# Ending a hand-made section ahead of the last store, with a second engine waiting for the earlier stores

## The chip, the cores and the metric

The kernel runs on one core of one Trainium2 chip. The metric is the device time in microseconds (us) of one execution. Every kernel here was executed several times, and its median is quoted. The record marks all executions quoted as fast: none lies over 1.5% above the fastest of its kernel. The profile of a kernel is that of one execution; its "span" runs from the first to the last instruction and is about 2 us shorter than the measured time.

## The reference

Sixteen independent products of a transposed 512 x 512 matrix with another, in float32:

```python
def setup_inputs():
    batch, m, k, n = 16, 512, 512, 512
    return {"a": randn(batch, k, m), "b": randn(batch, k, n)}       # float32

def reference(a, b):
    return np.matmul(a.transpose(0, 2, 1), b).astype(np.float32)
```

Inputs and outputs together are 50.33 MB: 33.55 MB are read and 16.78 MB written.

## The kernel before

The kernel takes two of the sixteen products at a time ("pairs", eight of them). SyncE issues all the DMAs, on one queue: sixteen loads of 2 MB, then eight stores of 2 MB. VectorE casts to bf16, TensorE multiplies, ScalarE copies the results from PSUM to the output tiles. The fifth engine, GpSimd, has no part in the products. All of this stands in one hand-made section (`tile_critical`), in which the author places every semaphore (a counter that one engine or DMA raises and another waits for); outside such a section the framework places them. The parts that matter here:

```python
    NX = 4                       # load buffers
    NO = pairs - 1               # 7 output tiles for 8 pairs
    ...
    with tc.tile_critical(no_gpsimd_drain=True):
        for n in range(2 * pairs):
            if n >= NX:
                nc.sync.wait_ge(s_in, n - NX + 1)
            nc.sync.dma_start(x_ts[n % NX][:], in_v[n % 2][n // 2]).then_inc(s_x[n % NX], 16)
        for i in range(pairs):
            nc.sync.wait_ge(s_out, i + 1)
            nc.sync.dma_start(out_v[i], o_ts[i % NO][:]).then_inc(s_o if i else s_o0, 16)
        nc.sync.wait_ge(s_o0, 16)                  # the waits at the section's end
        nc.sync.wait_ge(s_o, 16 * (pairs - 1))
        ...                                        # VectorE: casts; TensorE: matmuls
        for i in range(pairs):
            if i == NO:
                nc.scalar.wait_ge(s_o0, 16)        # store 0 has left its tile
            ...                                    # ScalarE: copies of PSUM to o_ts[i % NO]
            nc.scalar.memzero(act_done[:, i:i + 1]).then_inc(s_out, 1)
```

When a section ends, the framework adds an exit. In the compiled program of this kernel, SyncE announces that it has left; TensorE, VectorE, ScalarE and SyncE each drain (wait until their own earlier work is done) when they see this, and answer; SyncE collects the four answers. Then come the program's last instructions: a drain on SyncE that waits for what is still outstanding, and two rounds of a barrier of all engines with the clearing of the semaphores between them.

## Time and profile before

| | before |
|---|---|
| time, median of 3 runs | 124.58 us (124.52 to 124.60) |
| span of the profiled run | 122.5 us |
| bytes moved, mean rate over the span | 50.33 MB, 411 GB/s |
| share of the span in which the DMA engines are busy | 97.3% |
| last compute instruction ends | 94.5 us |
| last store complete ("last landing") | 121.11 us |
| from there to the end of the span ("tail") | 1.40 us |

A DMA here runs on sixteen DMA engines, and each of them adds one to the DMA's semaphore when its share is done. "Landing" below is always the moment of the sixteenth. The prediction shows the lines of this profile that carry the argument, with how to read them. In rows such as `L71 SPq EVENT_SEMAPHORE  x1: 17/17/17, 121.1 to 121.1` the three numbers are the shortest, median and longest duration in nanoseconds, and the last two the start of the first and the last of the group in microseconds; a q after the engine's name marks its sequencer. These views round to 0.1 us. Where I give more digits, they are start times and completion times of the same trace, which holds nanoseconds.

### The profile page before, as it was taken

The numbers are of one execution on the slowest core, as the hardware profiler recorded it, in microseconds if no ns is written. First come the engines' busy times: TensorE is split into PE (matmuls) and PEld (weight loads), VectorE is DVE, ScalarE is ACT, GpSimd is POOL, SyncE is SP. The second block draws the span as 40 slices with busy tenths as digits, with TensorE's granted clock in tenths as the row PEclk, the third lists the DMA queues.
The fourth block names the chain that finished last, engine by engine and source line by source line (L and its number), as shares of the span: only waits on it lengthen the run. The fifth ranks groups of instructions, "written<-read, shape, count | busy, mean of one in ns | idle before, by whom it ended". The sixth has DMA issues, their size and how long they took to land. (4 is left out here: it accounts for less than half of the span.)

```text
span 122.5 us, 1252 instructions
## 1 busy us (share of the span) xinstructions
PE 62.0 (51%) x512; PEld 35.8 (29%) x512; DVE 37.9 (31%) x48; ACT 31.8 (26%) x41; POOL 0.2 (0%) x4
## 2 busy tenths in 40 slices
PE   0000099889469659839919969947991000000000
PEld 0000045466146336426504536614560000000000
DVE  0012552574194094084265447429000000000000
ACT  4000000651910930740560083190038000000000
POOL 0000000000000000000000000000000000000000
PEclk9999999999999999999985999997799555555555
DMA  4999999999999999999999999999999999999992
GB/s 80 396 428 433 433 428 433 433 433 428 428 428 428 428 428 428 428 428 428 428 428 428 433 428 428 428 399 431 428 423 431 428 425 431 428 428 428 428 428 120
DMA packets 4480, 50.33 MB, mean 411 GB/s; under 512 B 384, under 2 KB 384, under 8 KB 384
## 3 DMA queue, kind: packets, MB, share of 16 engines
q1 hardware_dynamic: 4480, 50.33, 97.3%
HBM read 33.55 MB, written 16.78 MB: 411 GB/s over the span
## 5 line engine op out<-in xcount | busy, mean ns | idle before, releaser
L103 PE MATMUL ps<-bbf,abf 64*128 64x512 bf16 x512 | 62.0, 401 | 30.3 <-PEq L98 30.3
L103 PEld LDWEIGHTS ps<-bbf,abf 64*128 64x128 bf16 x512 | 35.8, 113 | 56.1 <-issue 39.4
L121 ACT COPY o<-ps 128x1024 f32<-128x1024 f32 x32 | 30.1, 1027 | 61.8 <-PE ps L103 61.8
L82 DVE CAST abf<-x 128x2048 bf16<-128x2048 f32 x16 | 19.6, 1224 | 24.1 <-PE ps L103 15.5
L82 DVE CAST bbf<-x 128x2048 bf16<-128x2048 f32 x16 | 19.6, 1225 | 23.5 <-DMA x<-in_b_dram 23.5
L126 ACT ACTIVATE act_done<-act_done 1x1 uint32<-1x1 uint32 x8 | 1.6, 196 | 0.0
L121 ACT ACT_TABLE_LOAD x1 | 1.3, 1283 | 0.9 <-SPq L62 0.9
L88 DVE MEMSET dve_done<- 1x1 f32 x16 | 0.9, 59 | 0.0
L141 POOL MEMSET const-bfloat16-1.0<- 128x1 bf16 x1 | 0.1, 102 | 0.0
L141 POOL MEMSET const-uint8-127<- 128x1 uint8 x1 | 0.1, 101 | 0.0
L141 POOL MEMSET const-float32-0.0<- 128x1 f32 x1 | 0.1, 99 | 0.2 <-issue 0.2
L141 POOL MEMSET const-float32-1.0<- 128x1 f32 x1 | 0.1, 98 | 0.0
## 6 DMA issues: line engine op xcount, KB each, us to landing
x<-in_a_dram SPq DMA_DIRECT2D x8, 2048.0 KB, 12.2
x<-in_b_dram SPq DMA_DIRECT2D x8, 2048.0 KB, 16.0
out_dram<-o SPq DMA_DIRECT2D x8, 2048.0 KB, 30.9
```

The costliest lines, as they stand in the source:

```text
L82: nc.vector.tensor_copy(out=(bbf_ts if n % 2 else abf_ts)[v][:], in_=x_ts[n % NX][:, v * RV:(v + 1) * RV, :],).then_inc(s_cast, 1)
L88: nc.vector.memset(dve_done[:, n:n + 1], 0.0).then_inc(s_in, 1)
L103: mm = nc.tensor.matmul(ps_ts[g][h][:, t % 2, :], a_m[:, t], bbf_ts[v][rows, r, :], start=(v == 0 and r == 0), stop=(v == V - 1 and r == R ...
L121: ev = nc.scalar.copy(out=o_ts[i % NO][:, g, 2 * h:2 * h + 2, :], in_=ps_ts[g][h][:])
L126: nc.scalar.memzero(act_done[:, i:i + 1]).then_inc(s_out, 1)
L141: nc = _bacc.Bacc("TRN2", target_bir_lowering=False, num_devices=1)
```

## The change

The intent is to get the section's exit out of the way of the end. The section ends once the seventh store (store 6) is issued. The last store is issued after it, outside any section, so the framework waits for it at the program's end. Somebody must still wait for stores 0 to 6, which carry the author's semaphores: GpSimd does, alone, in a second section. A scheduling fence (`no_sync_barrier`) keeps the order in which the framework places the two.

```diff
@@ the first section
-        for i in range(pairs):
+        for i in range(pairs - 1):
             nc.sync.wait_ge(s_out, i + 1)
             nc.sync.dma_start(out_v[i], o_ts[i % NO][:]).then_inc(s_o if i else s_o0, 16)
-        nc.sync.wait_ge(s_o0, 16)
-        nc.sync.wait_ge(s_o, 16 * (pairs - 1))
@@ behind it
+    with tc.tile_critical(sync_engine=mybir.EngineType.Pool, no_gpsimd_drain=True):
+        nc.gpsimd.wait_ge(s_o0, 16)
+        nc.gpsimd.wait_ge(s_o, 16 * (pairs - 2))
+    tc.no_sync_barrier()
+    nc.sync.dma_start(out_v[pairs - 1], o_ts[(pairs - 1) % NO][:])
```

## The prediction

> **What bounds the kernel now.** I read the page's part on slices first, to see which resource is full and until when.
>
> ```profile
> PE   0000099889469659839919969947991000000000
> ...
> DMA  4999999999999999999999999999999999999992
> GB/s 80 396 428 433 433 428 433 433 433 428 428 428 428 428 428 428 428 428 428 428 428 428 433 428 428 428 399 431 428 423 431 428 425 431 428 428 428 428 428 120
> ...
> q1 hardware_dynamic: 4480, 50.33, 97.3%
> ```
>
> The DMA engines are full from the second slice to the last but one, at 425 to 433 GB/s, on one queue. TensorE is done after slice 31 of 40, so nothing the compute engines do sets the end. The 50.33 MB at 428 GB/s take 117.6 us; with the start-up that is the span, 122.5 us. The measured 124.58 us holds some 2.1 us more that lie outside the span, and I leave those as they are.
>
> Next the stretches before and after the last byte: columns are the busy us of PE, PEld, DVE, ACT and POOL, then the granted clock, the DMA share and the GB/s.
>
> ```profile
> 94.90:121.00 26.10, 0.00 (x0) 0.00 (x0) 0.00 (x0) 0.00 (x0) 0.00 (x0) 0.50 0.98 417
> 121.00:122.50 1.50, 0.00 (x0) 0.00 (x0) 0.00 (x0) 0.00 (x0) 0.00 (x0) 0.50 0.00 0
> ```
>
> For 26 us the core only writes out what is queued. Then 1.5 us pass in which no engine computes and no byte moves. The chain of waits on the page does not show this: it ends with ScalarE at 94.5 us, 28 us before the span does. The queue's own waits and the timeline of SyncE show what is there.
>
> ```profile
> SPq L71 <- DMA out_dram<-o: 26.2, 1, 26.2
> ```
> ```profile
> 94.52 0.37 SPq L69 DMA_DIRECT2D out_dram<-o  x1
> ...
> DMA to landing us min/median/max: 26.6/26.6/26.6
> ```
>
> The last store is issued at 94.5 us, needs 0.37 us of SyncE, and lands 26.6 us later, because some five stores lie ahead of it in the queue. SyncE waits all that time at line 71. The trace's completion counts of the stores reach their sixteen at 91.8, 96.7, 101.6, 106.5, 111.4, 116.25 and 121.11 us for stores 1 to 7: one store every 4.88 us.
>
> Last the tail itself, by line, with the instruction's duration in ns and its first and last start. Line 62 is the section's own entry and exit, line 152 the end of the program.
>
> ```profile
> L71 SPq EVENT_SEMAPHORE  x1: 17/17/17, 121.1 to 121.1; - x1
> L66 SPq COMPARE_BRANCH  x1: 33/33/33, 121.2 to 121.2; - x1
> ...
> L62 SPq EVENT_SEMAPHORE  x1: 17/17/17, 121.3 to 121.3; - x1
> L62 ACTq DRAIN  x1: 8/8/8, 121.4 to 121.4; - x1
> ...
> L62 SPq DRAIN  x1: 7/7/7, 121.4 to 121.4; - x1
> ...
> L62 SPq EVENT_SEMAPHORE  x1: 28/28/28, 121.6 to 121.6; - x1
> L62 SPq NOP  x1: 13/13/13, 121.6 to 121.6; - x1
> ...
> L152 SPq DRAIN  x1: 7/7/7, 121.7 to 121.7; - x1
> ...
> L152 SPq DRAIN  x1: 7/7/7, 121.8 to 121.8; - x1
> ...
> L152 SPq EVENT_SEMAPHORE  x1: 17/17/17, 122.5 to 122.5; - x1
> ```
>
> The trace has these starts to the nanosecond. The landing is complete at 121.112 and the wait of line 71 passes at 121.129. SyncE branches out of the section at 121.193 and announces that at 121.348; the other engines drain on that at 121.387 to 121.394, SyncE at 121.443. SyncE collects their answers with waits at 121.522 and 121.575 and a NOP at 121.642. Only then comes the program's end: SyncE's first drain at 121.722, its drain into the final barrier at 121.785, two rounds of that barrier with the clearing of the semaphores between them, and the end at 122.526. So the tail of 1.41 us has two parts: the section's exit, 121.129 to 121.722, 0.59 us, and the program's end, 121.722 to 122.526, 0.80 us.
>
> **What the Trainium skill says.** "Perfetto Trace Analysis", section "Sequencer-only Instruction (DRAIN, etc)": such an instruction's reported start is when its semaphores are satisfied, and neither the wait nor the spread of its update is in the reported window. The trace agrees: the drains last 7 to 10 ns, but one step of the exit follows the other by 60 to 80 ns and the branch by 155, so I count steps start to start. "DMA: Bandwidth & Descriptors", section "Anatomy of one DMA — SWDGE (gpsimd) path": the DMA engines wait on no semaphore, the sequencer does before it issues, and a transfer carries about 2 us of fixed cost, mostly in completion. For this kernel's hardware-issued queue the first load took 7.7 us against a pace of 4.88 us, so 2.8 us of fixed cost; the measurement counts. Same page, "Queues, rings and completion order": a DMA engine takes a queue's descriptors in ring order. The evenly spaced landings agree; hence a store issued a little later, but still behind others, lands no later. Same page, "Where 436 GB/s comes from": 435 GB/s is the fabric's ceiling, which 428 to 433 nearly reaches, so nothing is left to gain in the stream.
>
> **The change part by part.**
> 1. Removed: SyncE's two waits at the section's end. The section now ends when SyncE has issued store 6 and the engines have finished. From the trace: SyncE's stores before the last begin at 66.4 us and the one at 83.8 us takes 4.65 us, so SyncE would leave at about 88.5 us. ScalarE's last instruction, which the exit must await, ends at 94.5 us. The section's exit, worth 0.59 us, thus moves from after 121.1 us to about 94.5 us, beside the store stream. This is the gain.
> 2. Moved: the last store now follows the exit. Instead of 94.52 us it starts about 94.5 + 0.6 = 95.1, with the branch perhaps 95.3 us. The store before it has been in the queue since 88.5 and occupies the engines until 116.25 us. The slack is 116.25 - 95.3 - 2.8 (fixed cost) = 18 us. Cost: nothing.
> 3. Added: GpSimd's section with two waits, passed at 116.25 us with store 6. Its exit costs about the same 0.6 us, so it is done by 117 us, 4 us before the last landing. Nothing on the path. The scheduling fence between it and the store adds an order, not a semaphore wait, as I read it; SyncE and GpSimd have separate instruction streams.
> 4. Added: the framework must wait for the last store itself, on a semaphore of its own, at the program's end. That wait takes line 71's place at about 121.13 us and is followed by the final barrier drain. If the end collects several semaphores (the store, GpSimd's section, SyncE's section) and the store's comes first, up to two further steps of 65 ns follow. More semaphores to clear: 18 took 136 ns, so one to three more are about 0.02 us.
> Sum: the path from the landing to SyncE's barrier drain was 121.785 - 121.112 = 0.67 us. It becomes 0.02 + 0.065 + (0 to 0.13) = 0.08 to 0.22 us. The gain is 0.45 to 0.59 us, less 0.02; I take 0.53. 124.58 - 0.53 = 124.05 us, 0.4% less.
>
> **The rivals.**
> A. The last store is held until GpSimd's section is over. If the framework turns the order of the two sections and the store into a real wait, the store starts not at 95 but at 116.25 + 0.1 to 0.7 us. The queue is then empty and the fixed cost is laid bare: landing 7.7 us later, at 124.05 to 124.65; plus 0.08 to 0.22 and the barrier's 0.74, the span is 124.9 to 125.6 us and the time 127.0 to 127.7 us, 1.9 to 2.5% slower. For it: the second section stands ahead of the store in the text. Against it: the store needs only ScalarE's result, and that belongs to the first section; GpSimd's section touches no tile. I give it 4%.
> B. No gain: the program's end gets as many handovers as the section's exit had, because it now has two sections and an outstanding store to collect. For it: the exit's cost was a chain of small steps, and steps can reappear. Against it: the other engines and GpSimd have been idle for microseconds by then, so their answers already stand, and in the trace of before the ones already answered cost a step of 65 ns and no more. Time 124.4 to 124.6 us. 12%.
> C. The stream itself slows or speeds up because the store comes from outside the section. It has the same tiles, size and queue; I see nothing for it.
>
> **Range and chances.** The main case gives 124.0 to 124.15; runs of before scatter by 0.08 us. With B on the upper side the range is 123.9 to 124.5 us. Faster by over 2% would need under 122.1 us, which would take stream time away: 0.5%. Slower by over 2% is over 127.1 us, most of A: 3%. Within 2%: 96.5%.
>
> **What would show it.** In the profile after: SyncE's last store starts near 95 us, and takes about 26 us to land (step 2; near 116.5 us and under 8 us would be A). The DMA row stays full to the end and the last landing stays at 121.1 us. The drains of the first section's exit stand at about 94.6 us rather than 121.4 (step 1). GpSimd has a wait that passes at 116.3 us (step 3). From the last landing to the span's end pass 0.82 to 0.98 us instead of 1.41 (step 4), and the span is 122.0 us. The prediction is wrong if the landing moves, or if that tail stays above 1.2 us (B).

## The result and the profile after

| | before | after |
|---|---|---|
| time, median of 6 runs each | 124.57 us (124.39 to 124.60) | 124.12 us (124.02 to 124.20) |
| ratio, 95% interval | | 0.9965 (0.9953 to 0.9978) |
| span of the profiled run | 122.5 us | 122.2 us |
| last store issued | 94.52 us | 93.10 us |
| last landing | 121.11 us | 121.26 us |
| tail | 1.40 us | 0.90 us |

The ratio is the mean time of the one kernel's fast runs over that of the other's fast runs in the same rounds, so it is not quite the ratio of the medians quoted. The interval is clear of 1, and the gain is 0.35% or 0.45 us.

The stream of transfers is what it was. From the page of the kernel after:

```profile
DMA  4899999999999999999999999999999999999993
GB/s 97 376 440 429 440 435 429 429 429 429 429 429 429 429 429 429 424 435 418 429 424 429 429 429 424 429 400 429 429 427 429 429 427 429 424 429 429 427 429 166
...
q1 hardware_dynamic: 4480, 50.33, 97.6%
```

The DMA engines are full from the third slice to the last but one, at the same rate. The two stretches from the last store's issue to its landing and from there to the end (columns as in the prediction):

```profile
93.10:121.25 28.15, 0.00 (x0) 0.00 (x0) 0.00 (x0) 0.00 (x0) 0.00 (x0) 0.55 0.98 414
121.25:122.20 0.95, 0.00 (x0) 0.00 (x0) 0.00 (x0) 0.00 (x0) 0.00 (x0) 0.50 0.00 0
```

Where 1.5 us without work or bytes stood before, there is now a little under 1 us. The waits of SyncE's queue say what became of the wait of 26.2 us:

```profile
SPq L157 <- DMA out_dram<-o: 27.7, 1, 27.7
...
SPq L62 <- PEq L62: 2.1, 1, 2.1
SPq L62 <- ACTq L62: 2.1, 1, 2.1
```

It is now a wait of line 157, the program's end, and not of the section. SyncE waits 2.1 us each for TensorE and ScalarE at line 62, the first section's exit; this is in the middle of the store stream and costs nothing. The last store, line 131:

```profile
L131 SPq DMA_DIRECT2D out_dram<-o x1: 373/373/373, 93.1 to 93.1; - x1
...
DMA to landing us min/median/max: 28.2/28.2/28.2
```

And the exit and the tail, by line (62 is the first section, 157 the program's end):

```profile
L62 DVEq DRAIN  x1: 10/10/10, 88.5 to 88.5; - x1
...
L62 ACTq DRAIN  x1: 2146/2146/2146, 90.9 to 90.9; - x1
L62 SPq NOP  x1: 13/13/13, 93.0 to 93.0; - x1
...
L157 POOLq EVENT_SEMAPHORE  x3: 17/43/23091, 93.2 to 93.3; - x3
...
L157 POOLq COMPARE_BRANCH  x1: 32/32/32, 116.5 to 116.5; - x1
...
L157 SPq EVENT_SEMAPHORE  x1: 28/28/28, 121.3 to 121.3; - x1
L157 SPq DRAIN  x1: 7/7/7, 121.3 to 121.3; - x1
...
L157 SPq DRAIN  x1: 7/7/7, 121.4 to 121.4; - x1
...
L157 SPq EVENT_SEMAPHORE  x1: 17/17/17, 122.1 to 122.1; - x1
```

The exit's drains now stand at 88.5 to 90.9 us and its last step at 93.0 us. GpSimd's long wait starts at 93.3 us and GpSimd leaves its section at 116.5 us. Two of these records contain a wait, unlike those in the tail, of which the prediction says that the wait lies outside the record: GpSimd's 23,091 ns are one instruction that waits for two semaphores, and ScalarE's drain of 2146 ns ends at 92.998 us, 0.04 us after ScalarE's last instruction. Behind the landing at 121.256 us only three steps of SyncE are left before the barrier: the wait passes at 121.272, a drain at 121.340, the drain into the barrier at 121.400. That is 0.144 us from the landing to this drain; before it was 0.673 us (121.112 to 121.785). The rest of the tail, from this drain to the end, is 0.760 us against 0.730: clearing 21 semaphores took 157 ns where clearing 18 took 136.

So the tail is 0.50 us shorter. The landing in this one profile is 0.14 us later, but the first load's is too, by 0.12 (8.75 us against 8.63); it is the start of the stream that differs between executions. The six runs of after have a mean span of 122.15 us, so with a tail of 0.90 a mean landing of 121.25 us. For the kernel before, the nine runs beside the first four experiments give 122.58 - 1.40 = 121.18 us.

### The profile page after: what moved, and what is told of

Read it like the earlier page. It is cut to its first block, busy times and chain, and to the rows that moved or that the text cites. A ratio compares the mean times of both kernels' runs of the same rounds, so it can differ in the third digit from the quotient of the medians.

```text
span 122.2 us, 1261 instructions
## 1 busy us (share of the span) xinstructions
PE 62.9 (51%) x512; PEld 35.9 (29%) x512; DVE 38.0 (31%) x48; ACT 31.8 (26%) x41; POOL 0.2 (0%) x4
## 5 line engine op out<-in xcount | busy, mean ns | idle before, releaser
L101 PE MATMUL ps<-bbf,abf 64*128 64x512 bf16 x512 | 62.9, 404 | 27.9 <-PEq L96 27.9
```

What stands on the lines that cost most here:

```text
L101: mm = nc.tensor.matmul(ps_ts[g][h][:, t % 2, :], a_m[:, t], bbf_ts[v][rows, r, :], start=(v == 0 and r == 0), stop=(v == V - 1 and r == R ...
```

## The experiments

The theory (E) is that the gain is the section's exit, moved from behind the last landing to a place where only the DMA engines are waited for. The rivals: (W) that it is GpSimd's taking over of the waits that pays; (S) that the gain has to do with how the last store is issued or lands, outside the section and with the framework's semaphore; and rival A of the prediction, a hold-up of the store, which the result has ruled out for the change but not measured.

Each run is named by a label, and was timed beside the kernel before on the same chip. "Tail" and "landing" are those of its profile.

| run | time, median | ratio to before, 95% interval | last landing | tail |
|---|---|---|---|---|
| second_exit | 125.73 us | 1.0097 (1.0081 to 1.0112) | 121.17 | 2.33 |
| pool_waits | 124.35 us | 0.9985 (0.9972 to 0.9999) | 121.21 | 1.17 |
| sp_section | 124.45 us | 0.9989 (0.9975 to 1.0003) | 121.54 | 1.26 |
| act_section | 124.11 us | 0.9965 (0.9952 to 0.9978) | 121.01 | 0.88 |
| late_store | 124.19 us | 0.9964 (0.9951 to 0.9977) | 121.60 | 0.90 |
| strict_order | 126.23 us | 1.0125 (1.0110 to 1.0140) | 123.40 | 0.90 |
| hold_store | 126.24 us | 1.0127 (1.0112 to 1.0141) | 122.91 | 1.39 |
| hidden_exit | 124.61 us | 1.0001 (0.9987 to 1.0015) | 121.76 | 0.90 |
| after_again | 124.13 us | 0.9966 (0.9952 to 0.9979) | 121.07 | 0.90 |
| hidden_again | 124.50 us | 1.0003 (0.9990 to 1.0017) | 121.40 | 0.90 |
| hidden_three | 124.58 us | 1.0001 (0.9988 to 1.0015) | 121.56 | 0.90 |
| pe_longer | 124.09 us | 0.9971 (0.9958 to 0.9985) | 121.11 | 0.90 |

### second_exit: one more exit behind the landing

The edit, on the kernel before:

```diff
+    tc.no_sync_barrier()
+    with tc.tile_critical(no_gpsimd_drain=True):
+        nc.sync.wait_ge(s_o, 16 * (pairs - 1))
+        nc.vector.wait_ge(s_o, 16 * (pairs - 1))
+        nc.tensor.wait_ge(s_o, 16 * (pairs - 1))
+        nc.scalar.wait_ge(s_o, 16 * (pairs - 1))
```

> The kernel before with one more hand-made section behind the first, in which SyncE, VectorE, TensorE and ScalarE each wait for the last store, which has landed by then. Theory E (the gain is the time that a section's exit takes after the last landing): one more entry and exit stand behind the landing, so the tail from the last landing to the end of the span grows from 1.41 us by the exit of 0.59 us plus an entry of 0.1 to 0.2, to 2.0 to 2.3 us, and the time is 0.6 to 0.9 us over the kernel before, about 125.3 us. Rival W (the gain is that GpSimd instead of SyncE waits) and rival S (the gain is in how the last store is issued and lands): nothing of theirs is touched, so 124.6 us.

The time rose by 1.2 us. From the views of single lines, the first section's wait and last exit step, then the second section's last exit step (line 128) and SyncE's first drain at the program's end:

```profile
L71 SPq EVENT_SEMAPHORE  x1: 17/17/17, 121.2 to 121.2; - x1
...
L62 SPq NOP  x1: 13/13/13, 121.7 to 121.7; - x1
...
L128 SPq NOP  x1: 13/13/13, 122.7 to 122.7; - x1
...
L158 SPq DRAIN  x1: 7/7/7, 122.7 to 122.7; - x1
```

The first exit took from 121.185 to 121.698 us, the second section's entry, waits and exit from there to 122.661, almost 1 us more. The tail grew by 0.93 us, to 2.33, just above the 2.0 to 2.3 that E expected; W and S expect nothing. The time rose by more than the 0.6 to 0.9 us expected. A further 0.17 us lies outside the span: time less span is 2.14 us on average in these runs and 1.97 in those of the kernel before. The rest, 0.09 us, is a later mean landing (mean span 123.60 us less the tail of 2.33, against 121.18). The part outside the span I had not foreseen; it comes back below.

### pool_waits: GpSimd waits, but in the one section

The edit, on the kernel before:

```diff
-        nc.sync.wait_ge(s_o0, 16)
-        nc.sync.wait_ge(s_o, 16 * (pairs - 1))
+        nc.gpsimd.wait_ge(s_o0, 16)
+        nc.gpsimd.wait_ge(s_o, 16 * (pairs - 1))
```

> The kernel before with its two end waits given to GpSimd, in the one section, so that GpSimd and not SyncE waits for all the stores. Rival W: 124.1 us, as the change. Theory E: the section still ends after the last landing. SyncE leaves it early, but whether the exit is early too depends on GpSimd's answer, for which the exit waits: the last steps (GpSimd's branch and answer, SyncE's collecting NOP, its drain) remain behind the landing. I work these out as a branch step of 0.155 and 0.065, and some three steps of 0.07 to 0.08, 0.45 us in place of 0.67, so 124.3 to 124.5 us: part of the gain, not all.

124.35 us: part of the gain, as E expected, and not the whole, as W did. GpSimd's wait and branch, its answer, SyncE's collecting NOP and the drain into the barrier:

```profile
L71 POOLq EVENT_SEMAPHORE  x1: 17/17/17, 121.2 to 121.2; - x1
L66 POOLq COMPARE_BRANCH  x1: 33/33/33, 121.3 to 121.3; - x1
L62 POOLq NOP  x1: 13/13/13, 121.5 to 121.5; - x1
L62 SPq NOP  x1: 13/13/13, 121.5 to 121.5; - x1
...
L152 SPq DRAIN  x1: 7/7/7, 121.6 to 121.6; - x1
```

The other engines' answers were given long before; those that hang on GpSimd still stand behind the landing. From the landing at 121.208 to the drain into the barrier at 121.637 us it is 0.43 us, between the 0.67 of before and the 0.14 of after. The tail, 1.17 us, is 0.23 shorter than before's; the time fell by 0.18. The intervals of this run and of the change just touch (0.9972 to 0.9999 and 0.9953 to 0.9978), so it is the traced steps more than the time that speak against W.

### sp_section: the second section on SyncE

The edit, on the kernel after:

```diff
-    with tc.tile_critical(sync_engine=mybir.EngineType.Pool, no_gpsimd_drain=True):
-        nc.gpsimd.wait_ge(s_o0, 16)
-        nc.gpsimd.wait_ge(s_o, 16 * (pairs - 2))
-    tc.no_sync_barrier()
     nc.sync.dma_start(out_v[pairs - 1], o_ts[(pairs - 1) % NO][:])
+    tc.no_sync_barrier()
+    with tc.tile_critical(sync_engine=mybir.EngineType.SP, no_gpsimd_drain=True):
+        nc.sync.wait_ge(s_o0, 16)
+        nc.sync.wait_ge(s_o, 16 * (pairs - 2))
```

> The changed kernel with the second section on SyncE in place of GpSimd, put behind the last store's issue. The compiled program shows that the end of this section then waits for the last store as well, since SyncE issued it before. Theory E: a short exit of one engine is back behind the landing, about 0.5 us from the landing to the final barrier drain where the change has 0.14 and the kernel before 0.67, so 124.4 to 124.5 us. If an early end of the first section were all that matters: 124.1 us.

124.45 us, as expected, and no longer clear of the kernel before. SyncE's steps behind the landing at 121.544 us:

```profile
L157 SPq EVENT_SEMAPHORE  x1: 28/28/28, 121.6 to 121.6; - x1
L157 SPq COMPARE_BRANCH  x1: 33/33/33, 121.6 to 121.6; - x1
...
L129 SPq NOP  x1: 13/13/13, 121.9 to 121.9; - x1
L157 SPq DRAIN  x1: 7/7/7, 122.0 to 122.0; - x1
```

The wait ahead of the branch, the first line, is for the last store's semaphore too. So the exit of this one-engine section is back on the path: 0.52 us from the landing to the drain into the barrier at 122.064. The late landing of this profile is that of its execution, the slowest of five (124.78 us); from the five spans, 122.52 us on average, less the tail of 1.26 us the mean landing is 121.26 us. This run also speaks against S: here too the last store is issued outside the first section, with the framework's semaphore, and the gain is gone.

### act_section: the second section on ScalarE

The edit, on the kernel after:

```diff
-    with tc.tile_critical(sync_engine=mybir.EngineType.Pool, no_gpsimd_drain=True):
-        nc.gpsimd.wait_ge(s_o0, 16)
-        nc.gpsimd.wait_ge(s_o, 16 * (pairs - 2))
+    with tc.tile_critical(sync_engine=mybir.EngineType.Activation, no_gpsimd_drain=True):
+        nc.scalar.wait_ge(s_o0, 16)
+        nc.scalar.wait_ge(s_o, 16 * (pairs - 2))
```

> The changed kernel with the second section on ScalarE instead of GpSimd, in the same place, ahead of the last store. Theory E: any engine but SyncE will do, 124.1 us, 0.4 per cent under the kernel before. Rival W in its narrow form (it is GpSimd that helps): back to about 124.5 us.

124.11 us and the same ratio as the change, 0.9965. It is not GpSimd alone that helps; ScalarE, waiting ahead of the last store in the framework's order, does as well. One of its six runs took 124.56 us although its span, 122.0 us, was like the others'; what happened there lies outside the span.

### late_store: how late the last store may be issued

The edit, on the kernel after; store 6 gets a semaphore of its own, since on a shared one the wait for store 5 could be met in part by completions of store 6:

```diff
+    s_o6 = tc.alloc_semaphore("s_o6")
...
-            nc.sync.dma_start(out_v[i], o_ts[i % NO][:]).then_inc(s_o if i else s_o0, 16)
+            nc.sync.dma_start(out_v[i], o_ts[i % NO][:]).then_inc(
+                s_o0 if i == 0 else s_o6 if i == pairs - 2 else s_o, 16
+            )
+        nc.sync.wait_ge(s_o, 16 * 5)
...
-        nc.gpsimd.wait_ge(s_o, 16 * (pairs - 2))
+        nc.gpsimd.wait_ge(s_o, 16 * (pairs - 3))
+        nc.gpsimd.wait_ge(s_o6, 16)
```

> The changed kernel, but SyncE waits in the first section for store 5 to land (store 6 has a semaphore of its own so that this wait is unambiguous), so the section ends at about 111.5 us and the last store is issued at about 112.1 us instead of 93.1. Theory: store 6 still keeps the DMA engines busy until 116.4 us, and the 2.8 us of fixed cost fit in the 4.3 us that are left, so the last landing and the time stay, 124.1 us. If the place of the store's issue mattered before the queue runs dry: above 124.3 us.

The last store, line 136 here:

```profile
L136 SPq DMA_DIRECT2D out_dram<-o x1: 372/372/372, 112.4 to 112.4; - x1
...
DMA to landing us min/median/max: 9.2/9.2/9.2
```

The store was issued at 112.36 us, 19 us later than in the change, and the section's exit stood at 111.8 to 112.3 us. The ratio is 0.9964, that of the change. The exit and the store may thus stand as late as this, 4.3 us before store 6 lands at 116.70 us, without a cost; nothing between this and an empty queue was tried. (The landing of its profile is late from the start: its first load landed at 9.09 us.) This also speaks against S: between 93 and 112 us the time of the store's issue is of no account.

### strict_order and hold_store: what rival A would have cost

Strict_order, on the kernel after:

```diff
-    tc.no_sync_barrier()
+    tc.strict_bb_all_engine_barrier()
```

> The changed kernel with the scheduling fence between GpSimd's section and the last store made a real barrier: rival A of the prediction. The store should start at about 117.0 us, 0.6 us after store 6 landed at 116.4; it lands 7.7 us later if it costs what the first load cost, at 124.7 us, and with the tail of 0.92 us the span is 125.6 us and the time 127.5 us, 2.4 per cent over the kernel before.

Hold_store, on the kernel before:

```diff
             nc.sync.wait_ge(s_out, i + 1)
+            if i == pairs - 1:
+                nc.sync.wait_ge(s_o, 16 * (pairs - 2))
```

> The kernel before, with one more wait: SyncE issues the last store only once store 6 has landed, at 116.3 us. It separates the fixed cost of a store issued into an empty queue from the hand-over of a section. The store starts at 116.35 us and lands 7.7 us later, 124.05, in place of 121.1: 2.9 us slower, 127.5 us. Against strict_order, this has the exit of 0.5 us behind the landing in place of 0.6 us between the two stores, so both should come out nearly alike.

Both are slower by about 1.25%, alike as expected, but by 1.6 us and not by 2.9. The last store of strict_order:

```profile
L131 SPq DMA_DIRECT2D out_dram<-o x1: 373/373/373, 117.0 to 117.0; - x1
...
DMA to landing us min/median/max: 6.4/6.4/6.4
```

With no other transfer outstanding, the 2 MB store landed after 6.40 us here and 6.43 us in hold_store, not after the 7.7 us of the first load. Over the pace of 4.89 us this is 1.5 us. In addition the sixteen completions of this store came within 0.19 us (123.21 to 123.40), while those of the change's last store, which ran close behind the others, were spread over 0.71 us (120.55 to 121.26). The mechanism of rival A was right, and its size was not.

### hidden_exit, and three runs about it

The edit, on the kernel after: the same additional section as in second_exit, ahead of the last store.

```diff
+    with tc.tile_critical(no_gpsimd_drain=True):
+        nc.sync.wait_ge(s_out, pairs)
+        nc.vector.wait_ge(s_out, pairs)
+        nc.tensor.wait_ge(s_out, pairs)
+        nc.scalar.wait_ge(s_out, pairs)
+    tc.no_sync_barrier()
     with tc.tile_critical(sync_engine=mybir.EngineType.Pool, no_gpsimd_drain=True):
```

> The changed kernel with the same additional four-engine section put between the first section and GpSimd's, so at about 94 us, ahead of the last store's issue. Theory E: its entry and exit lie beside the store stream, the last store starts about 0.7 to 1 us later with some 18 us to spare, and the time stays that of the changed kernel, 124.1 us, 0.4 per cent under the kernel before. If sections cost time wherever they stand, it loses the 0.6 to 0.9 us, 124.8 us.

This missed: 124.61 us, the whole gain lost. Yet the steps it moved are where they should be. The additional section stood at 93.1 to 94.0 us, the last store was issued at 94.09 us, and the tail is 0.905 us as in the change. The last landing was late, 121.76 us. I ran it again on another chip, with the change as a control, with a three-engine variant that has no wait of TensorE, and with a variant that only lengthens TensorE's program:

```diff
# hidden_three, on the kernel after
+    with tc.tile_critical(no_gpsimd_drain=True):
+        nc.sync.wait_ge(s_out, pairs)
+        nc.vector.wait_ge(s_out, pairs)
+        nc.scalar.wait_ge(s_out, pairs)
+    tc.no_sync_barrier()
# pe_longer, on the kernel after, at the end of TensorE's part of the first section
+        for _ in range(8):
+            nc.tensor.wait_ge(s_out, 1)
```

> The changed kernel unaltered, as the control on the chip of the next three runs. 124.1 us, a tail of 0.90 us from the last landing to the end, and spans that scatter by 0.1 us.

> The run hidden_exit once more, on another chip. It came out at 124.61 us though its tail was 0.905 us, as the change's: its last landing was late, 121.76 us in place of 121.26, because one of the sixteen completions of each store trailed the others by 0.6 us from store 1 on. If that is the chance of one execution, the median here goes to 124.1 to 124.3 us. If the kernel does it, it stays at 124.5 to 124.7 us. Its profile also held one instruction fetch in mid-stream, at 97.4 us, that no other run had; if it is there again the kernel causes it.

> The additional section ahead of the last store with three engines only, without TensorE, so that TensorE's program grows by no waits. Theory E and the reading that the longer program's instruction fetch disturbs the stores: no fetch in mid-stream, 124.1 us. If a further section ahead of the last store costs time in itself: 124.5 us or more again.

> The changed kernel with eight satisfied waits at the end of TensorE's part of the first section and no further section. If it is TensorE's longer program that brings a fetch into the store stream and delays one DMA engine: a fetch between 90 and 100 us and 124.4 to 124.6 us. Otherwise 124.1 us; the waits themselves pass beside the store stream.

The control gave 0.9966 again. The loss is the kernel's: hidden_again 1.0003 and hidden_three 1.0001. Waits of TensorE are not needed for it (hidden_three has none in the additional section), and eight of them alone don't bring it: pe_longer kept the gain. What the three kernels with the additional section share, compared with the control, is worked out from the runs thus (span less tail is the landing; means of five runs):

| | mean time | mean span | mean landing | time less span |
|---|---|---|---|---|
| after_again | 124.06 us | 122.10 | 121.20 | 1.96 |
| hidden_exit | 124.62 us | 122.46 | 121.55 | 2.16 |
| hidden_again | 124.54 us | 122.42 | 121.52 | 2.12 |
| hidden_three | 124.55 us | 122.44 | 121.54 | 2.11 |

So the loss of about 0.5 us is 0.3 us of a later landing and 0.15 to 0.2 us outside the span. The stream was undisturbed up to the last load: from the sixteenth load's landing to the last store's it then took 39.36 to 39.56 us in the three profiles, and 39.10 us in the change's two and in pe_longer's. In the same three profiles, and in no other, an instruction fetch falls into the stores, at 97.4, 97.1 and 99.2 us; from the DMA queues of hidden_three:

```profile
q1 hardware_dynamic: 4480, 50.33, 97.4%
q14 instruction: 1, 0.01, 0.0%
```

In the other traces this fetch comes at 123 us or later, by when the last landing is past. That it marks a longer program is a guess, and the traces speak against it as the cause of the delay: it moves 8 KB in 0.31 us on one DMA engine, and most of the delay is older. Counted from the sixteenth load's landing, the store that lands at about 97 us is already 0.54 us later than in the change in hidden_exit, 0.35 in hidden_three and 0.23 in hidden_again, and the last store 0.46, 0.27 and 0.35. The profile of sp_section has the same delay, 39.45 us with stores late from 87 us on, and its fetch comes at 123.9 us. There it is one slow execution, whose run has a mean landing of 121.26 us; in the kernels with the additional section the mean itself is late. In these profiles one or two of a store's sixteen completions trail the others (by 0.57 us for store 1 in hidden_exit, 0.50 in sp_section). What delays them stays open.

So does what the time outside the span is spent on. It was longer by 0.15 to 0.2 us in the four kernels with an additional section of three or four engines, second_exit included (in act_section, without its one outlier, by 0.10). In these four the fetch lies inside the span (second_exit: 123.06 us); in all others it comes 1.1 to 1.4 us behind the span's end. Whether the two are linked was not tested. It is not the place of the first section's exit: late_store had that at 112 us and was no slower than the change.

No run beat the change clear of the noise; act_section, late_store and pe_longer equal it.

## Why the prediction was right

The predicted time was 124.05 us, measured were 124.12 and, in the control, 124.13; the range of 123.9 to 124.5 us holds both, and so did "within 2%". That range reaches into the times of rival B (124.4 to 124.6 us), so the time alone is a weak test; the tail decides, at 0.90 us, where 0.82 to 0.98 was predicted and over 1.2 meant B. Point by point, by the prediction's own steps:

1. **The exit leaves the tail.** Right, and shown. Its drains start at 88.5 to 90.9 us and not at the predicted 94.6, because SyncE announces the exit when it leaves, at 88.5, and each engine drains for itself; the last answer, ScalarE's, came only when its work was done, at 92.96 us. Second_exit shows the reverse: a further entry and exit behind the landing lengthened the tail by 0.93 us.
2. **The later store costs nothing.** Right, though its start was off by two microseconds: 93.10 us in place of 95.1 to 95.3. ScalarE happened to end at 92.96 us in this execution, and after it the exit needed only 0.14 us, because the other engines had answered by then; I had added the whole exit of 0.6 us. Late_store shows that the slack is there: 19 us later made no difference.
3. **GpSimd's section is off the path.** Right: it was over by 117 us, 4 us before the last landing. That it need not be GpSimd (act_section), must not be SyncE behind the store (sp_section), and does not suffice inside the one section (pool_waits) is shown by runs; the prediction had not said it.
4. **The program's end takes over the wait at 0.08 to 0.22 us.** It took 0.144 us from the landing to the drain into the barrier, with one further step of 68 ns behind the wait, and the clearing cost 0.02 us more, as worked out. The tail shrank by 0.50 us. The prediction's own terms, 0.45 to 0.59 less 0.02, have their middle at 0.50, and the 0.53 that it took leaves out the 0.02. The medians differ by 0.45 us; the 0.05 left over goes with the landing, which was to stay and on average came 0.07 us later (121.25 us against 121.18). That is within what the landings scatter.

Three readings in it are slightly off, without consequence: the span ends at 122.515 us and not 122.526, which makes the tail 1.40 us; SyncE's steps in the exit take 53 to 95 ns beside the branch's 155, not 60 to 80; and among the full slices some lie below 425 GB/s (396, 399 and 423).

Of the rivals, A would not have been slower by over 2%. Its mis-sized term is the fixed cost of a store into an empty queue, taken from the first load as 2.8 us over the pace: strict_order measured 1.5 us, and the time would have been 126.2 us and not 127.0 to 127.7. The 3% for "slower" had therefore nothing to rest on. B, the handovers coming back at the program's end, did not happen in the change, but it is what sp_section has. C cannot be seen in the change; the hidden_exit runs show that a stream can be slowed without being touched in the source, by some 0.3 us, which I had not thought of.

## What to carry to other kernels

When a kernel ends on a full DMA queue, count the steps between the last landing and the end one by one: in this kernel each handover there was paid in full, while the first section's exit cost nothing as long as transfers were still queued. Issue the last transfer outside the hand-made section and let an engine that has nothing to do behind it wait for the rest, ahead of it in the framework's order. And check that an edit meant to be free really leaves the landing alone: one further section beside the stream cost this kernel 0.5 us.

## What the Trainium skill lacked or had wrong

- "DMA: Bandwidth & Descriptors", section "Anatomy of one DMA — SWDGE (gpsimd) path": the fit with a fixed cost of about 2 us was measured on GpSimd's queue, and no page has such a measurement for SyncE's. On SyncE's queue a 2 MB store with nothing else outstanding took 6.40 and 6.43 us, 1.5 us over the pace of 4.89, and the first load 7.7 us, 2.8 over it.
- The same page, "Where 436 GB/s comes from": its warning says, without a condition, that for transfers between HBM and SBUF the HBM side, about 358 GB/s, binds. This program on one core sustained 424 to 435 GB/s in most slices, for reads and for writes. The note further up on that page, which gives about 358 GB/s for two cores streaming at once, is not contradicted.
- The same page lacks how far the sixteen completions of one transfer lie apart: 0.52 to 1.14 us for the last of a train of stores (twelve profiles), 0.19 and 0.22 us for one with nothing else outstanding. The landing is the last of the sixteen.
- "Runtime: NRT & Kernel Launch", section "Instruction fetch mechanics", calls the crossing of an instruction block mostly hidden and has no duration for a fetch. A fetch of 8 KB among the stores, at 97 to 99 us in three kernels, took 0.31 us on one DMA engine; these kernels were slower, but most of their stores' delay is older than the fetch, so the page is not shown to be wrong.
- No page has the price of leaving and entering a hand-made section: an exit of four engines took 0.59 us behind the landing (branch to announcement 155 ns, SyncE's other steps 53 to 95 ns), entry, waits and exit of one more 0.96 us, an exit that waits for one other engine 0.43 us from the landing to the barrier in place of 0.67.
